# First mixer of a hybrid model block: float32 products on unsplit weights in place of three split products, modulation on TensorE, silu on ScalarE, the last projection by token halves

## The chip, the cores and the metric

One core of one Trainium2 chip runs the whole program. The metric is the device time of one execution in microseconds (us), lower is better. The times of a kernel are taken on several executions and their median is compared; the profile is of one execution of its own.

## What is computed

The input is 256 tokens of 1024 float32 features. The program has two blocks, each a mixer followed by a mixture of experts of its own kind (the first with 32 experts, four of them per token). All of it is float32. Only the first mixer concerns this study; cut to what matters:

```python
shift, scale, gate, ... = split(silu(c) @ ada_w + ada_b)         # modulation, 6 x 1024
h = rmsnorm(x, norm1_g) * (1 + scale) + shift
proj = h @ w_in                                     # gdn_qkv, gdn_z, ssd_z, ssd_xbc, small columns
qkv = silu(causal_dwconv(gdn_qkv, gdn_conv_w))      # four taps
q, k = l2norm(...), l2norm(...)
o = gated_delta_rule_chunked(q, k, v, beta, g)      # 4 chunks of 64 tokens, one after the other
o = rmsnorm(o, gdn_norm_g) * silu(gdn_z)
xbc = silu(causal_dwconv(ssd_xbc, ssd_conv_w) + ssd_conv_b)
y = ssd_chunked(...) + ssd_d * xs
y = rmsnorm(y * silu(ssd_z), ssd_norm_g)            # in two groups
x = x + gate * (concatenate([o, y]) @ w_out)
# then: norm2, router logits, experts
```

## The kernel before

The chip's engines work beside each other: TensorE (PE) multiplies matrices, VectorE (DVE), ScalarE (ACT) and GpSimd (POOL) do the rest, and the queue of SyncE (SP) issues the loads of weights. All weights come from HBM once, in chunks of 128 partitions x 2048 float32 (1 MB). The class `Stream` hands them out: a list `todo` in the order of use, a number of slots in SBUF, and a load is issued (L173) as soon as its turn has come and a slot of its phase (A is the first mixer, B its experts) is free. In phase A there are N1 = 4 slots; for phase B come six of ring1 when the mixer ends and five of the pool pB, 15 in all.

*Start (0 to about 36 us).* `ada_first` (L448 and around) computes the first third of the modulation on PE: for each of eight chunks four matmuls of 512 columns, each in a group of 32 of the array's columns, summed over the chunks. Meanwhile x is normalised and transposed to `h32`.

*Projections.* The mixer has 34 projection chunks: 6 for the SSD convolution input, 8 for q and k, 4 for ssd_z, 4 for v, 4 for gdn_z, 4 + 4 for the output. Each is 256 output columns wide and makes 16 products (8 blocks of the contraction by two halves). PE has a fast format, fp32r, with fewer bits; to keep the accuracy both operands are split in a high and a low part. `splitter` (L364 and around) does this for a weight chunk in four parts: ACT copies a part into `wh` in fp32r, then DVE or POOL (the table SPD says which) makes `wl` = w - wh. `h` is split in the same way into `hT`, and the inputs of the output projection into the pairs `cs` and `cg`. One product is then three fp32r matmuls:

```python
mm(o, l[0], r[0], start=start, stop=False)
mm(o, l[0], r[1], start=False, stop=False)
mm(o, l[1], r[0], start=False, stop=stop)
```

The slot of a chunk is given back when it is split, and one chunk is split ahead of use (`Stream.get`).

*Modulation batches 1 and 2* (`ada_batch`, L463): eight chunks each, multiplied and summed on DVE (L479, 128x2048 each), then a product with ones on PE adds over the partitions. They lie beside the projections.

*What follows a projection.* `conv_silu`: ACT takes the first tap from PSUM, DVE the three others (L661), ACT a tanh, DVE the last step (L664): silu(z) as (tanh(z/2) + 1) * z/2, with the halves folded into the weights. Then PE transposes the result, ACT copies it. For the two gates the same by `twice_silu` and in `emit_z`.

*Order.* It is set by generators that give up their turn at each piece: `weave` runs a main generator, and after each of its turns so much of the side generators as their rates say (FILL1, FILL2 for the projections beside a main chain, RA for the modulation). In turn: the SSD projections; the q and k projections beside `ssd`; `gdn_prep` (around L900 to L950), the inverse of 64x64 triangular blocks by doubling, in blocks of 32 (matmuls of Xc, Yc, Qc, with Xc the transposed of Yc by DVE, L927), beside ssd_z and v; `gdn_steps`, the chain over four chunks of 64 tokens, beside gdn_z and the SSD half of the output projection. What is left of the side work runs after the chain. Then the GDN outputs `o` are transposed, multiplied with norm weight and gate, split, and the GDN half of the output projection runs for both halves of the tokens (128 each) of each of four chunks; `router_logits` takes each result, adds it to x (L1202 transposes it) and multiplies with the router's weights. The experts' first product, `ps_gu<-w,xe`, follows at 426 us. Behind the mixer nothing is changed.

Of the kernel before, what the change touches and what calls it, by code (L numbers as in the profile page):

```python
# [12 lines left out]
F32 = mybir.dt.float32  # L13
# [104 lines left out]
class Stream:  # L118
# [151 lines left out]
def kernel_body(ctx, tc, ins, consts, out):  # L270
# [78 lines left out]
    pA = Sides(tc, "pA", {"a4", "wh", "wl", "vT", "cf", "gb0", "gh", "ssx", "jkx", "ss", "rsv", "rsq", "rs"})  # L349
# [4 lines left out]
    SP.dma_start(x, ins["x"].rearrange("o (t p) d -> p (o t) d", p=P))  # L354
    ws.ring(pw, N1 - 3, ph)

# [21 lines left out]
    ws.splitter = splitter(pA)  # L378
    k.spd = SPD[0]

# [82 lines left out]
    def ada_batch(b):  # L463
# [26 lines left out]
        ws.give(slot)  # L490
# [54 lines left out]
    nc.vector.tensor_scalar(col_w, pb[:, :144], 0.5, None, op0=ALU.mult)  # L545
    hb = pA.tile([P, 12], F32, name="hb")
    nc.vector.tensor_scalar(hb, colv("ssd_conv_b"), 0.5, None, op0=ALU.mult)
# [16 lines left out]
    ws.ring(pB, N2 - NR1, {"B": N2 - NR1})  # L564
    block1_moe(k, pB)
    ws.close(pB)
    pB_cm.__exit__(None, None, None)
    ps_cm.__exit__(None, None, None)
# [18 lines left out]
def mixer1(k):  # L587
    nc, tc, ws, pA = k.nc, k.tc, k.ws, k.pA
    mm, mm3, tt, act, bank, C, ident = k.mm, k.mm3, k.tt, k.act, k.bank, k.C, k.ident
    Cb = k.Cb  # L590
    split_into = k.split_into
    hT, h32, ro, col_w, hb, colv = k.hT, k.h32, k.ro, k.col_w, k.hb, k.colv
# [5 lines left out]
    def a4r(name):  # L598
        return pA.tile([P, 1024], F32R, tag="a4", bufs=NA4, name=name)
# [52 lines left out]
    def conv_silu(pj, wc, ct, nct, dst, bias=None):  # L652
# [9 lines left out]
        th = pA.tile([P, T], F32, tag="cv_t", bufs=2, name="cv_t")  # L662
        act(th, y, AF.Tanh)
        V.scalar_tensor_tensor(dst, th, 1.0, y, op0=ALU.add, op1=ALU.mult)  # L664

    def proj_ch(n, emit, emit2=None):

        for i in range(n):
            w = ws.get(split=True)
# [14 lines left out]
    def proj_tok(n, l, emit):  # L684

        for i in range(n):
            w = ws.get(split=True)
            pj = bank("pj", PJ)
            for t in range(2):
                for kk in range(KD):  # L690
                    sl = slice(kk * 256, kk * 256 + 256)
# [1838 lines left out]
```

## Time and profile before

| | |
|---|---|
| time, median of 3 executions | 2185.27 us (2173.07 to 2186.01) |
| the profiled execution's own time | 2186.19 us |
| its span (first to last instruction) | 2184.4 us |
| first mixer, from the start to the first gate_up product | 426 us |
| PE busy, over the span | 89% |
| DVE / ACT / POOL busy, over the span | 32% / 20% / 12% |
| HBM read | 703.70 MB |

The span and the time differ by what lies before and after the first and last instruction. PE busy means that a matmul was under way, at whichever clock; the granted clock is a mean over a stretch, as a share of full speed. The rows come from one execution.

### The profile page before, as it was taken

How to read it: one execution, taken by the hardware profiler on the slowest of the kernel's cores; microseconds unless marked ns; L12 is line 12 of the kernel's file. 1: busy time of each engine (PE TensorE's matmuls, PEld its weight loads, DVE VectorE, ACT ScalarE, POOL GpSimd, SP SyncE). 2: the span in 40 equal slices, each digit the busy share in tenths (PEclk: the TensorE clock that was granted, in tenths of full speed). 3: DMA queues.
4: the chain of work that ended last, by engine and by line, in shares of the span. 5: the costliest groups of instructions: out<-in, count | busy, mean ns of one | idle time of the engine just before them, and what ended most of it. 6: DMA issues, size and time to landing. Idle time of an engine off the chain costs nothing. (4 is left out here: it accounts for less than half of the span.)

```text
span 2184.4 us, 27466 instructions
## 1 busy us (share of the span) xinstructions
PE 1942.8 (89%) x11276; PEld 1035.2 (47%) x11277; DVE 695.8 (32%) x1438; ACT 436.5 (20%) x1030; POOL 256.9 (12%) x206
## 2 busy tenths in 40 slices
PE   6888899799999999989999999879999887776777
PEld 3877878633343434334343333378779531212111
DVE  4988847421111111111211111374765200001001
ACT  3655424211010101001010000132444210101001
POOL 2524212100000000000000000242434000000000
PEclk9999879999999999999999999989999899998999
DMA  8654415789999999988999999926238699999997
GB/s 309 212 174 136 150 66 174 293 349 391 411 420 421 421 421 406 388 363 353 414 418 416 422 393 422 359 92 193 78 87 334 273 420 421 420 421 371 421 421 290
DMA packets 170747, 706.67 MB, mean 324 GB/s; under 512 B 20775, under 2 KB 83796, under 8 KB 95860
## 3 DMA queue, kind: packets, MB, share of 16 engines
q1 hardware_dynamic: 170612, 704.80, 81.4%
q8 instruction: 93, 1.52, 0.3%
q14 instruction: 42, 0.34, 0.0%
HBM read 703.70 MB, written 1.05 MB: 323 GB/s over the span
## 5 line engine op out<-in xcount | busy, mean ns | idle before, releaser
L283 PE MATMUL ps_gu<-w,xe 128*64 128x512 f32 (+1 forms) x3072 | 693.0, 629 | 82.2 <-DMA w<-in_w_up_dram 36.6
L283 PEld LDWEIGHTS ps_gu<-w,xe 128*64 128x64 f32 (+1 forms) x3072 | 228.9, 132 | 524.7 <-issue 398.0
L283 PE MATMUL ps_y<-w,aT 128*64 128x512 f32 (+1 forms) x1536 | 383.9, 599 | 13.8 <-DMA w<-in_w_down_dram 13.0
L283 PEld LDWEIGHTS ps_y<-w,aT 128*64 128x64 f32 (+1 forms) x1536 | 116.5, 127 | 234.0 <-issue 182.9
L293 POOL TENSOR_TENSOR wl<-w,wh 128x512 fp32r<-128x512 f32 x126 | 179.5, 1433 | 387.1 <-ACT wh L296 382.8
L1579 DVE TENSOR_SCALAR g<-ps_gu 128x512 f32<-128x512 f32 x32 | 22.0, 686 | 490.2 <-PE ps_gu L283 490.2
L296 ACT ACTIVATE g<-g 128x512 f32<-128x512 f32 x32 | 20.2, 630 | 694.7 <-DVE g L1579 694.7
L296 ACT ACTIVATE wh<-w 128x512 fp32r<-128x512 f32 x244 | 139.4, 622 | 88.1 <-PE ps_pj L283 51.9
L283 PE MATMUL ps_pj<-hT,wh 128*128 128x256 f32 x704 | 146.4, 304 | 7.5 <-DVE cv_y L661 3.5
L293 DVE TENSOR_TENSOR wl<-w,wh 128x512 fp32r<-128x512 f32 x118 | 116.1, 1002 | 48.1 <-ACT wh L296 47.4
L283 PEld LDWEIGHTS ps_pj<-hT,wh 128*128 128x128 f32 x704 | 119.4, 205 | 13.4 <-issue 5.7
L293 DVE TENSOR_TENSOR x<-x,ps_g 128x512 f32<-128x512 f32 x96 | 66.0, 687 | 173.9 <-PE ps_g L283 173.9
L283 PE MATMUL ps_pj<-hT,wl 128*128 128x256 f32 x352 | 107.0, 304 | 4.9 <-DVE wl L293 2.5
L283 PE MATMUL ps_g<-ys,sgT 128*128 128x512 f32 x192 | 93.7, 617 | 1.7 <-DVE ys L293 0.8
L283 PE MATMUL ps_g<-selr,xo 128*128 128x256 f32 x320 | 76.7, 394 | 18.3 <-ACT selr L296 15.3
L293 DVE TENSOR_TENSOR a<-g,ps_gu 128x512 f32<-128x512 f32 x8 | 5.5, 687 | 239.3 <-PE ps_gu L283 239.3
L283 PEld LDWEIGHTS ps_g<-selr,xo 128*128 128x128 f32 x320 | 56.8, 192 | 47.8 <-ACT selr L296 23.3
L283 PEld LDWEIGHTS ps_pj<-hT,wl 128*128 128x128 f32 x352 | 72.6, 206 | 6.9 <-DVE wl L293 2.8
L283 PE MATMUL ps_pj<-uT,wh 128*128 128x256 f32 x384 | 72.8, 291 | 0.0
L283 PEld LDWEIGHTS ps_pj<-uT,wh 128*128 128x128 f32 x384 | 61.4, 197 | 4.2 <-issue 3.7
L293 DVE TENSOR_TENSOR ys<-ps_y,gb 128x512 f32<-128x512 f32 x32 | 22.1, 692 | 129.3 <-PE ps_y L283 129.3
L1381 DVE COPY aT<-ps_g 128x512 f32<-128x512 f32 x16 | 11.1, 692 | 159.2 <-PE ps_g L1376 159.2
(533 smaller groups left out, 2137.0 us busy)
## 6 DMA issues: line engine op xcount, KB each, us to landing
w<-in_moe_w_gu_dram SPq DMA_DIRECT2D x256, 1024.0 KB, 12.6
w<-in_moe_w_down_dram SPq DMA_DIRECT2D x120, 1024.0 KB, 16.2
w<-in_w_gate_dram SPq DMA_DIRECT2D x64, 1024.0 KB, 19.8
w<-in_w_up_dram SPq DMA_DIRECT2D x64, 1024.0 KB, 19.8
w<-in_w_down_dram SPq DMA_DIRECT2D x64, 1024.0 KB, 19.8
w<-in_w_in_dram SPq DMA_DIRECT2D x45, 1024.0 KB, 5.2
w<-in_ada_w_dram SPq DMA_DIRECT2D x24, 1024.0 KB, 5.1
w<-in_w_out_dram SPq DMA_DIRECT2D x12, 1024.0 KB, 6.1
```

What stands on the lines that cost most here:

```text
L283: return nc.tensor.matmul(o, l, r, start=start, stop=stop)
L293: (eng or nc.vector).tensor_tensor(o, a, b, op=op)
L296: nc.scalar.activation(o, i, f, **kw)
L1381: k.nc.vector.tensor_copy(dst, pt)
L1579: V.tensor_scalar(g, gu[j], 7.0, None, op0=ALU.min)
```

## The change

- The projections take the float32 chunk as it lies in its slot, and float32 activations: one matmul for each product in place of three. `wh`, `wl`, `hT` and the split pairs `cs`, `cg` are gone, and with them the work of `splitter` in this mixer (the second mixer keeps it, with the same values of SPD). A chunk keeps its slot until its products are issued.
- The two later modulation batches are made on PE like the first one: 64 matmuls of 512 columns, then four transposes and two products that pick a row.
- silu is one ScalarE function in place of tanh and a DVE step; the halves that were folded in are gone.
- A pool `pq` adds four slots to phases A and B (8 in A); pB has one slot in place of five, so that B has 15 as before. No more than four chunks are live until the small vectors (`rowsA`) are under way.
- The GDN half of the output projection runs by halves of the tokens: the first half (`first_tile`) beside the last steps of the chain, the second after it. Its four chunks keep their slots until the second half has used them. The router's logits are taken by halves, too. FILL2 is 1.05.

```diff
+    def raw(self):
+
+        self.fill()
+        return self._next("mm")
...
+    pq_cm = tc.tile_pool(name="pq", bufs=NQ)
+    pq = pq_cm.__enter__()
...
+    ws.limit(N1)
     ws.ring(pw, N1 - 3, ph)
+    ws.ring(pq, NQ, {"A": NQ, "B": NQ})
...
-        acc = None
+        pm = None
         for kk in range(KD):
             while not ws.ready():
                 yield
             w = ws.get()
-            if acc is None:
-                acc = w
-                slot = ws.take()
-                nc.vector.tensor_scalar(acc, w, cact[:, 0:1], None, op0=ALU.mult)
-            else:
-                nc.vector.scalar_tensor_tensor(acc, w, cact[:, kk:kk + 1], acc, op0=ALU.mult, op1=ALU.add)
-                ws.done()
+            pm = pm or bank()
+            for j in range(4):
+                mm(pm[32 * j:32 * j + 32], cb[:, kk], w[:, j * 512:(j + 1) * 512], start=(kk == 0), stop=(kk == KD - 1))
...
+        mr = pA.tile([P, 512], F32, tag="t2b", bufs=2, name="mr")
+        act(mr, pm, AF.Copy)
         pt = bank()
-        for j in range(8):
-            mm(pt[:, j:j + 1], acc[:, c0 + j * P:c0 + j * P + P], C("ones"))
-        tt(mcol[:, 8 + 8 * b:16 + 8 * b], pt[:, :8], colv("ada_b1")[:, 8 * b - 8:8 * b], ALU.add)
+        for q in range(4):
+            nc.tensor.transpose(pt[:, q * P:(q + 1) * P], mr[:, q * P:(q + 1) * P], ident)
+        v = lambda a: a.rearrange("p (j q) -> p q j", j=2)
+        tt(v(mcol[:, 8 + 8 * b:16 + 8 * b]), pt.rearrange("p (q j r) -> p q j r", q=4, r=32)[:, :, c0 // 512:c0 // 512 + 2, 0],
+           v(colv("ada_b1")[:, 8 * b - 8:8 * b]), ALU.add)
         for n in range(2):
+            r = 32 * (g0 // 512 + n)
             pg = bank()
-            mm(pg, Cb("ones"), acc[:, g0 + n * 512:g0 + n * 512 + 512])
+            mm(pg, ident[:, r:r + 1].to_broadcast([P, P]), mr)
...
+    ws.limit(99)
...
-    hT = [pA.tile([P, KD, T], F32R, name=f"hT{i}") for i in range(2)]
     for kk in range(KD):
         h = h32[kk // 4][:, kk % 4]
         nc.vector.tensor_scalar(h, h, a1[:, kk:kk + 1], mcol[:, kk:kk + 1], op0=ALU.mult, op1=ALU.add)
-        split_into(h, hT[0][:, kk], hT[1][:, kk], eng=nc.gpsimd if kk % 2 else None)
...
+    ws.ring(pB, NB, {"B": NB})
...
-        th = pA.tile([P, T], F32, tag="cv_t", bufs=2, name="cv_t")
-        act(th, y, AF.Tanh)
-        V.scalar_tensor_tensor(dst, th, 1.0, y, op0=ALU.add, op1=ALU.mult)
+        act(dst, y, AF.Silu)
...
-                    sl = slice(kk * 256 + ct * P, kk * 256 + ct * P + P)
-                    mm3(pj[:, ct * T:(ct + 1) * T], (w[0][:, sl], w[1][:, sl]), (hT[0][:, kk], hT[1][:, kk]), start=(kk == 0), stop=(kk == KD - 1))
+                    c0 = kk * 256 + ct * P
+                    mm(pj[:, ct * T:(ct + 1) * T], w[:, c0:c0 + P], h1(kk), start=(kk == 0), stop=(kk == KD - 1))
...
+            ws.give(slot)
...
-            g2 = twice_silu(pj)
+            g2 = pA.tile([P, 512], F32, tag="t2a", bufs=2, name="hs")
+            act(g2, pj, AF.Silu)
...
-            cf = pA.tile([P, T], F32, tag="cf", bufs=2, name="cf")
-            act(cf, pt[:, :T], AF.Copy, scale=colv("ssd_norm_g")[:, c:c + 1])
-            split_into(cf, cats[c // 4][0][:, c % 4], cats[c // 4][1][:, c % 4])
+            act(cats[c // 4][:, c % 4], pt[:, :T], AF.Copy, scale=colv("ssd_norm_g")[:, c:c + 1])
...
+                    done[0] = hg == 1
...
+        act(zs[i // 2][:, (i % 2) * 2:(i % 2) * 2 + 2], pj.rearrange("p (a b) -> p a b", a=2), AF.Silu)
...
+    def gdn_cat(t):
+        for hg in range(2):
+            pt = bank()
+            for i in range(4):
+                h = hg * 4 + i
+                nc.tensor.transpose(pt[:, i * P:(i + 1) * P], o[t][:, h * P:(h + 1) * P], C("swap"))
+            sl = slice(t * P, (t + 1) * P)
+            V.scalar_tensor_tensor(catg[hg][:, :, sl], pt.rearrange("p (c s) -> p c s", c=4), gh, zs[hg][:, :, sl], op0=ALU.mult, op1=ALU.mult)
+
+    def gdn_out(t, emit):
+        for i in range(4):
+            if t == 0:
+                c = ws.raw()
+                while c is None:
+                    yield
+                    c = ws.raw()
+                held.append(c)
+            w, slot = held[i]
+            pj = bank("pj", PJ)
+            for kk in range(KD):
+                mm(pj[:, :256], catg[kk // 4][:, kk % 4, t * P:(t + 1) * P], w[:, kk * 256:(kk + 1) * 256], start=(kk == 0), stop=(kk == KD - 1))
+            if t:
+                ws.give(slot)
+            emit(i, t, pj[:, :256])
+            yield
...
+    def first_tile():
+        yield from ada2
+        r.extend(router())
+        while not done[0]:
+            yield
+        catg.extend(catp("cg"))
+        gdn_cat(0)
+        yield
+        yield from gdn_out(0, r[0].tile)
+
+    r, done = [], [False]
+    fill = chain(proj_ch(4, None, emit_z), ssd_out, first_tile())
     weave(gdn_steps(), (fill, FILL2), (ada2, RA[3]))
-    run_all(fill, ada2)
+    run_all(fill)
...
-    k.spd = SPD[4]
...
-    catg = catp("cg")
-    for h in range(8):
...
-        split_into(cf, catg[h // 4][0][:, h % 4], catg[h // 4][1][:, h % 4])
...
-    emit, logits = router_logits(k, pA, add, lambda: pA.tile([P, 256], F32, tag="cf", bufs=2, name="xT"), k.rw, 32)
-    run_all(proj_tok(4, lambda part, kk, t: catg[kk // 4][part][:, kk % 4, t * P:(t + 1) * P], emit))
-    logits(k.lg, k.cr)
-
+    gdn_cat(1)
+    run_all(gdn_out(1, r[0].tile))
+    r[1](k.lg, k.cr)
...
+    def emit_t(i, t, o):
+        sl = slice(i * 256, (i + 1) * 256)
+        add(t, sl, o)
+        if t not in pl:
+            pl[t] = k.bank()
...
-SPD = ((1, 2),) * 3 + ((1, 2, 3), (1, 3), (), (1, 2), (1, 2))
+SPD = ((), (1, 2), (1, 2))
 RA = (0.34, 0.4, 0.25, 0.3)
 FILL1 = 0.8
-FILL2 = 0.6
+FILL2 = 1.05
 N1 = 4
-N2 = 11
+NQ = 4
+NB = 1
```

Three places show how the rows of the queues move. First DVE, in the doubling steps of the inverse: `Yc` is brought up to date, `Xc` is its transposed, which PE waits for; `cs`, `wl` are splits, `w<-w,cact` a step of the modulation, `cv_y` the taps of a convolution. Before:

```order
L293 TENSOR_TENSOR Yc<-Yc,ps_g 128x256
L293 TENSOR_TENSOR cs_2366<-cf,cs_2365 128x256 x2
L927 STREAM_TRANSPOSE Xc<-Yc 128x256
L479 SCALAR_TENSOR_TENSOR w<-w,cact 128x2048
L661 SCALAR_TENSOR_TENSOR cv_y<-ps_pj,col_w,cv_y 128x255
L293 TENSOR_TENSOR wl<-w,wh 128x512
L661 SCALAR_TENSOR_TENSOR cv_y<-ps_pj,col_w,cv_y 128x254
L293 TENSOR_TENSOR wl<-w,wh 128x512
L661 SCALAR_TENSOR_TENSOR cv_y<-ps_pj,col_w,cv_y 128x253
L664 SCALAR_TENSOR_TENSOR vT<-cv_t,cv_y 128x256
```

After:

```order
L294 TENSOR_TENSOR Yc<-Yc,ps_g 128x256
L933 STREAM_TRANSPOSE Xc<-Yc 128x256
L662 SCALAR_TENSOR_TENSOR cv_y<-ps_pj,col_w,cv_y 128x255
L662 SCALAR_TENSOR_TENSOR cv_y<-ps_pj,col_w,cv_y 128x254
L662 SCALAR_TENSOR_TENSOR cv_y<-ps_pj,col_w,cv_y 128x253
```

The transpose stands directly behind the update, and the splits, the modulation step and the last step of silu (L664) are gone from the queue.

Second PE, at the last GDN step (`vn,dT` is its last product): `cs` products are the SSD half of the output projection, `cg` the GDN half, `o` the chain's result, `rw,xT` the router's logits, `w,c_64` and `c_64,w` the sums over the partitions of a modulation batch. Before:

```order
L283 MATMUL ps_g<-c_64,w 128x1 x8
L283 MATMUL ps_g<-w,c_64 128x512 x2
L283 MATMUL ps_g<-vn,dT 64x128 x4
L283 MATMUL ps_pj<-wh,cs_2365 128x256
L283 MATMUL ps_pj<-wl,cs_2365 128x256
L283 MATMUL ps_pj<-wh,cs_2366 128x256
L283 MATMUL ps_pj<-wh,cs_2365 128x256
```

After:

```order
L284 MATMUL ps_g<-rw,xT 128x32 x2
L284 MATMUL ps_pj<-w,cg_2881 128x256 x3
L1232 MATMUL ps_g<-c_64,x 128x128 x2
L284 MATMUL ps_g<-vn,dT 64x128 x3
L284 MATMUL ps_g<-rw,xT 128x32 x2
L284 MATMUL ps_g<-vn,dT 64x128 x5
L1127 MATMUL ps_g<-ca,o_2394 128x128 x4
L284 MATMUL ps_pj<-w,cg_2880 128x256 x2
L1127 MATMUL ps_g<-ca,o_2394 128x128 x4
L284 MATMUL ps_pj<-w,cg_2880 128x256 x3
L284 MATMUL ps_pj<-w,cg_2881 128x256 x4
L284 MATMUL ps_pj<-w,cg_2880 128x256 x3
```

Before, the SSD half is still to come behind the last step and the GDN half behind that; after, the SSD half and most of the first token half of the GDN products lie ahead of the last step, and the second half follows it.

Third ACT, at the first convolutions: `cv_y` is the first tap, `cv_t` a tanh, `xT` a silu, `ea` an exponential, `sp_e` and `sp_z` the exponential and logarithm of the softplus; ACT_TABLE_LOAD loads the functions that the next activation needs. Before:

```order
L296 ACTIVATE cv_y<-ps_pj,hb,col_w 128x256
L296 ACTIVATE cv_t<-cv_y 128x256
L296 ACTIVATE cv_y<-ps_pj,hb,col_w 128x256
L296 ACTIVATE ea<-rowsA 128x24
L296 ACTIVATE cv_t<-cv_y 128x256
L296 ACTIVATE cv_y<-ps_pj,hb,col_w 128x256
L296 ACTIVATE sp_e<-sp_e 128x64
L296 ACT_TABLE_LOAD
L296 ACTIVATE sp_z<-sp_u 128x64
L296 ACT_TABLE_LOAD
L296 ACTIVATE cv_t<-cv_y 128x256
L296 ACTIVATE cv_y<-ps_pj,hb,col_w 128x256
```

After:

```order
L297 ACTIVATE cv_y<-ps_pj,col_a,col_w 128x256
L297 ACT_TABLE_LOAD
L297 ACTIVATE xT<-cv_y 128x256
L297 ACTIVATE cv_y<-ps_pj,col_a,col_w 128x256
L297 ACT_TABLE_LOAD
L297 ACTIVATE ea<-rowsA 128x24
L297 ACT_TABLE_LOAD
L297 ACTIVATE xT<-cv_y 128x256
L297 ACT_TABLE_LOAD
L297 ACTIVATE sp_e<-sp_e 128x64
L297 ACTIVATE cv_y<-ps_pj,col_a,col_w 128x256
L297 ACT_TABLE_LOAD
```

In this piece six loads stand where two stood; up to the experts' first product the queue has 20 where it had 5.

## Rows read from the trace of the kernel before

**Rows 1.** The page's first part: busy us, share of span, instructions of each engine.

```profile
PE 1942.8 (89%) x11276; PEld 1035.2 (47%) x11277; DVE 695.8 (32%) x1438; ACT 436.5 (20%) x1030; POOL 256.9 (12%) x206
```

**Rows 2.** Windows by stage: start:end, us, PE PEld DVE ACT POOL busy, PEclk, DMA, GB/s.

```profile
0.00:36.00 36.00, 17.64 (x86) 5.49 (x88) 9.31 (x29) 11.18 (x22) 4.33 (x9) 1.00 0.94 354
36.00:196.00 160.00, 141.96 (x1005) 126.05 (x1005) 137.69 (x246) 90.73 (x252) 63.84 (x47) 0.93 0.56 184
196.00:290.00 94.00, 79.21 (x1833) 72.64 (x1833) 74.85 (x132) 37.68 (x90) 33.34 (x22) 0.90 0.46 148
290.00:364.00 74.00, 74.00 (x508) 62.58 (x506) 41.07 (x110) 28.95 (x79) 10.57 (x7) 0.85 0.25 84
364.00:414.00 50.00, 44.68 (x358) 41.97 (x356) 33.38 (x76) 17.53 (x47) 12.61 (x9) 1.00 0.66 255
414.00:426.00 12.00, 4.81 (x24) 4.08 (x24) 7.69 (x46) 2.80 (x9) 2.15 (x2) 0.70 0.83 338
```

**Rows 3.** Windows of 10 us around the end of the mixer and in the experts.

```profile
400.00:410.00 10.00, 9.28 (x76) 8.83 (x76) 4.35 (x8) 2.32 (x9) 1.02 (x1) 1.00 0.30 109
480.00:490.00 10.00, 10.00 (x28) 2.57 (x30) 3.29 (x6) 0.00 (x0) 0.00 (x0) 0.66 0.46 161
560.00:570.00 10.00, 10.00 (x48) 3.98 (x45) 0.00 (x0) 0.00 (x0) 0.00 (x0) 1.00 1.01 421
```

**Rows 4.** Waits of PE, 0 to 435 us: total us, times, longest us.

```profile
PE ps_g L283 <- DMA w<-in_ada_w_dram: 9.6, 5, 3.5
PE ps_g L809 <- DVE qk L664: 5.7, 3, 4.6
...
PE ps_pj L283 <- ACT hT L296: 3.2, 1, 3.2
```

**Rows 5.** Groups of instructions, 36 to 196 us: busy us, mean ns, idle before.

```profile
L293 POOL TENSOR_TENSOR wl<-w,wh 128x512 fp32r<-128x512 f32 x33 | 49.4, 1501 | 89.5 <-ACT wh L296 85.6 <-PE ps_pj L283 4.0
L296 ACT ACTIVATE wh<-w 128x512 fp32r<-128x512 f32 x65 | 38.1, 626 | 8.7 <-PE ps_pj L283 6.5 <-issue 1.7 <-DMA w<-in_w_in_dram 0.4
L293 DVE TENSOR_TENSOR wl<-w,wh 128x512 fp32r<-128x512 f32 x34 | 32.9, 977 | 2.1 <-ACT wh L296 1.5 <-issue 0.6
L479 DVE SCALAR_TENSOR_TENSOR w<-w,cact 128x2048 f32<-128x2048 f32 x7 | 16.4, 2341 | 0.0
```

**Rows 6.** Timeline of PE, out-projection: start us, us, engine line op.

```profile
404.14 0.40 PE L283 MATMUL ps_pj<-wh,cg 128*128 128x256 f32 x2
404.38 0.28 PE L283 MATMUL ps_pj<-wl,cg 128*128 128x256 f32 x1
...
407.67 0.28 PE L283 MATMUL ps_pj<-wh,cg 128*128 128x256 f32 x1
```

**Rows 7.** Timeline of PE in the expert stage: a train of float32 products.

```profile
515.17 5.57 PE L283 MATMUL ps_g<-selr,xo 128*128 128x256 f32 x24
520.57 0.61 PE L1310 MATMUL ps_g<-c,sg 128*128 128x128 f32 x4
```

**Rows 8.** The same train as a window (columns as in rows 2).

```profile
515.17:520.57 5.40, 5.40 (x25) 4.19 (x25) 0.00 (x0) 2.82 (x5) 0.00 (x0) 1.00 1.02 419
```

**Rows 9.** Timeline of PE in the start: chunks of the first modulation batch.

```profile
9.71 1.94 PE L283 MATMUL ps_g<-w,cb 128*32 128x512 f32 x8 [0.44 <-DMA w<-in_ada_w_dram]
...
26.34 1.92 PE L283 MATMUL ps_g<-w,cb 128*32 128x512 f32 x16
```

**Rows 10.** Timeline of PE in the GDN steps: small matmuls between products.

```profile
309.32 0.43 PE L283 MATMUL ps_g<-r,Y 64*64 64x128 f32 x2
309.68 0.38 PE L283 MATMUL ps_pj<-hT,wh 128*128 128x256 f32 x1
309.91 0.28 PE L283 MATMUL ps_pj<-hT,wl 128*128 128x256 f32 x1
```

**Rows 11.** Timeline of ACT at the softplus.

```profile
56.66 1.28 ACT L296 ACT_TABLE_LOAD   x1
57.96 0.26 ACT L296 ACTIVATE sp_z<-sp_u 128x64 f32<-128x64 f32 x1
```

**Rows 12.** Timeline of PE where the first mixer ends.

```profile
426.08 8.48 PE L283 MATMUL ps_gu<-w,xe 128*64 128x512 f32 x32
```

More of the change, by code (lines that the diff above doesn't have):

```diff
@@ L544, in kernel_body @@
     nc.tensor.transpose(pb[:, 96:144], sw2, ident[:48, :48])
-    nc.vector.tensor_scalar(col_w, pb[:, :144], 0.5, None, op0=ALU.mult)
-    hb = pA.tile([P, 12], F32, name="hb")
-    nc.vector.tensor_scalar(hb, colv("ssd_conv_b"), 0.5, None, op0=ALU.mult)
+    nc.vector.tensor_copy(col_w, pb[:, :144])
     a2 = pc.tile([P, KD], F32, name="a2")
@@ L596, in a4, with h1 @@
         return pA.tile([P, 1024], F32, tag="a4", bufs=NA4, name=name)
-    def a4r(name):
-        return pA.tile([P, 1024], F32R, tag="a4", bufs=NA4, name=name)
+    def h1(kk):
+        return h32[kk // 4][:, kk % 4]
     pb = bank()
@@ L661, in conv_silu, with chunks @@
             V.scalar_tensor_tensor(y[:, s:], pj[:, :T - s], w(3 - s), y[:, s:], op0=ALU.mult, op1=ALU.add)
-        th = pA.tile([P, T], F32, tag="cv_t", bufs=2, name="cv_t")
-        act(th, y, AF.Tanh)
-        V.scalar_tensor_tensor(dst, th, 1.0, y, op0=ALU.add, op1=ALU.mult)
-    def proj_ch(n, emit, emit2=None):
-        for i in range(n):
-            w = ws.get(split=True)
+        act(dst, y, AF.Silu)
+    def chunks(n):
+        for i in range(n):
+            c = ws.raw()
+            while c is None:
+                yield None
+                c = ws.raw()
+            yield i, *c
+    def proj_ch(n, emit, emit2=None):
+        for c in chunks(n):
+            if c is None:
+                yield
+                continue
+            i, w, slot = c
             pj = bank("pj", PJ)
@@ L684, in proj_tok @@
     def proj_tok(n, l, emit):
-        for i in range(n):
-            w = ws.get(split=True)
+        for c in chunks(n):
+            if c is None:
+                yield
+                continue
+            i, w, slot = c
             pj = bank("pj", PJ)
@@ L953, in catp @@
     def catp(nm):
-        return [[a4r(f"{nm}{i}{p}").rearrange("p (c s) -> p c s", c=4) for p in range(2)] for i in range(2)]
+        return [a4(f"{nm}{i}").rearrange("p (c s) -> p c s", c=4) for i in range(2)]
     cats = []
@@ L967, in emit @@
                     act(jk, ys[t][:, g * 512:(g + 1) * 512], AF.Square, accum_out=ssy[:, t * 2 + g:t * 2 + g + 1])
-        yield from proj_tok(4, lambda part, kk, t: hT[part][:, kk, t * P:(t + 1) * P], emit)
+        yield from proj_tok(4, lambda kk, t: h1(kk)[:, t * P:(t + 1) * P], emit)
         rsy = pA.tile([P, 4], F32, name="rsy")
-        k.rstd(rsy, ssy, 0.25 / 512, pA, "rsy")
+        k.rstd(rsy, ssy, 1.0 / 512, pA, "rsy")
         for t in range(2):
@@ new lines, in mixer1, with add, router @@
+    gh = colv("gdn_norm_g")
+    catg, held = [], []
+    def add(t, sl, o):
+        d = pA.tile([P, 256], F32, tag="vT", bufs=2, name="d")
+        tt(d, o, gb[0][:, sl])
+        tt(x[:, t, sl], x[:, t, sl], d, ALU.add)
+    def router():
+        V.scalar_tensor_tensor(k.a2, k.mcol[:, 24:32], 1.0, colv("norm2_g"), op0=ALU.add, op1=ALU.mult)
+        pt = bank()
+        for kk in range(KD):
+            mm(pt[:, :32], k.mcol[:, 16 + kk:17 + kk].to_broadcast([P, P]), k.rw[:, kk], start=(kk == 0), stop=(kk == KD - 1))
+        tt(k.cr, pt[:, :32], k.rb, ALU.add)
+        tt(k.rw, k.rw, k.a2[:, :, None].to_broadcast([P, KD, 32]))
+        return router_logits(k, pA, add, lambda: pA.tile([P, 256], F32, tag="cf", bufs=2, name="xT"), k.rw, 32)
@@ L1148, in cols @@
     def cols(w, c0, n):
-        return [(w[:, c:c + 256].rearrange("(k p) n -> p k n", p=P), (8, 256), None, True) for c in range(c0, c0 + n, 256)]
+        return [(w[:, c:c + 256].rearrange("(k p) n -> p k n", p=P), (8, 256), None, "mm") for c in range(c0, c0 + n, 256)]
     def mixed(main, side, every):
@@ L1192, in router_logits @@
     x, nc = k.x, k.nc
-    pl = [k.bank() for _ in range(2)]
+    pl = {}
     ssx = pool.tile([P, 2, 4], F32, name="ssx")
+    def emit_t(i, t, o):
[3 more added lines that the diff above has]
+            pl[t] = k.bank()
+        pt = k.bank()
+        for j in range(2):
+            nc.tensor.transpose(pt[:, j * P:(j + 1) * P], x[:, t, i * 256 + j * P:i * 256 + j * P + P], k.ident)
+        xT = tile()
+        if t:
+            k.act(xT, pt[:, :256], AF.Copy)
+        else:
+            nc.vector.tensor_copy(xT, pt[:, :256])
+        for j in range(2):
+            mi = k.mm(pl[t][:, :n], xT[:, j * P:(j + 1) * P], rw[:, i * 2 + j], start=(i == 0 and j == 0), stop=(i == 3 and j == 1))
+        k.act(tile(), x[:, t, sl], AF.Square, accum_out=ssx[:, t, i:i + 1])
+        if i == 3 and t and WARM2[0]:
+            k.warm(WARM2[0], mi, k.ca[:, 0:512])
     def emit(i, pj):
-        sl = slice(i * 256, (i + 1) * 256)
         for t in range(2):
-            add(t, sl, pj[:, t * 256:(t + 1) * 256])
-            pt = k.bank()
-            for j in range(2):
-                nc.tensor.transpose(pt[:, j * P:(j + 1) * P], x[:, t, i * 256 + j * P:i * 256 + j * P + P], k.ident)
-            xT = tile()
-            if t:
-                k.act(xT, pt[:, :256], AF.Copy)
-            else:
-                nc.vector.tensor_copy(xT, pt[:, :256])
-            for j in range(2):
-                mi = k.mm(pl[t][:, :n], xT[:, j * P:(j + 1) * P], rw[:, i * 2 + j], start=(i == 0 and j == 0), stop=(i == 3 and j == 1))
-            k.act(tile(), x[:, t, sl], AF.Square, accum_out=ssx[:, t, i:i + 1])
-        if i == 3 and WARM2[0]:
-            k.warm(WARM2[0], mi, k.ca[:, 0:512])
+            emit_t(i, t, pj[:, t * 256:(t + 1) * 256])
+    emit.tile = emit_t
     def logits(dst, bias):
```

70 lines of the change are left out of this document (21 added, 49 removed).

## Prediction

> **What bounds the kernel now.** I read the page's busy shares first: TensorE (PE) works 89% of the span [rows 1], so the question is whether it is PE's work or its waits that set the changed stretch. The table by stage comes next [rows 2]. The change touches only the first mixer, which ends where the first expert's gate_up product starts, at 426 us. Up to 36 us the DMA is the limit (share 0.94). From 36 to 414 us PE is busy 141.96 + 79.21 + 74.00 + 44.68 = 339.9 of 378 us: 38 us of waits, and the rest work, part of it at the low clock (granted 0.93, 0.90, 0.85, 1.00). VectorE (DVE) is nearly as full in the first of these stages, 137.69 of 160 us. The list of what PE waits for [rows 4] names the culprits: modulation weights from HBM 9.6 us, the silu result qk on DVE 5.7 us, the split of hT 3.2 us, and many small ones.
>
> Does a shift of the mixer's end reach the total? In the expert stage the weights stream at 421 GB/s, but at 400 to 410 and at 480 to 490 us the DMA share is only 0.30 and 0.46 [rows 3]: the weight slots are full and the stream stands still until PE has used one. So I let a microsecond of the mixer be a microsecond of the total. The profiled execution took 2186.19 us, 0.9 above the median of 2185.27; the sum is made against 2186.19. About 1% (21.9 us) is what a measurement of this kernel tells from no change.
>
> **Part by part.**
>
> *Products.* 34 chunks of 16 products each = 544. Before, one product is three fp32r records: ten products lie between 404.14 and 407.67 us [rows 6], 0.353 us each. After, it is one float32 product, two records of 256 columns each. The expert stage shows this shape: 24 records from 515.17 to 520.57 [rows 7], 0.450 a product; the window's own row counts 25 records [rows 8], by which it is 0.432. I take 0.44: 544 x (0.44 - 0.353) = +47 us (bounds +43 and +53).
>
> *Modulation on PE.* Two batches of eight chunks leave DVE, where one chunk is a 128x2048 instruction of 2.34 us [rows 5], and go to PE, four 512-column matmuls in four column groups. The first batch already does it so: two chunks in 1.92 us at the high clock, one in 1.94 at the low one [rows 9]. 16 x 0.96 = +15 us (bounds +15 and +31); the transposes and the row products that follow take the place of 16 products with a vector of ones and two of 512 columns, and are set at nothing.
>
> *Waits that go.* The split went over ScalarE (ACT), DVE and GpSimd (POOL): from 36 to 196 us 65 copies by 0.626 on ACT, 34 subtractions by 0.977 on DVE, 33 by 1.50 on POOL, and 7 modulation steps [rows 5]. DVE gets 33 + 16 = 49 us lighter in that stage alone, ACT 38. The order shows what PE's operands stood behind: in the inverse two splits stand between the update of Yc and its transposed Xc, which PE needs for the next doubling, and behind Xc a modulation step of 2.34 us and two wl splits among the taps of the convolution; after, nothing stands between and the taps follow each other. Of the 38 us I take three quarters away, -29 (bounds 0 and -38): the waits for the dependent chain itself (convolution, silu, transpose) stay.
>
> *Clock.* A granted mean of 0.93 lies between two levels, 1.2 and 2.4 GHz; the time at the lower is 2 x (0.07 x 160 + 0.10 x 94 + 0.15 x 74) = 63 us [rows 2], which costs at most half, 32. The granted clock was 1.00 where PE had products close together, 364 to 414 us, and less where small matmuls or waits filled the time. With denser work I take back half: -16 (bounds 0 and -32).
>
> *Small matmuls between products.* From 308.4 to 311.9 products and pairs of 64-row matmuls alternate, and the product after such a pair takes 0.38 where its neighbour takes 0.28 [rows 10], 0.1 more. The order has as many such changes after as before (212 for 214 in the mixer), so I take -4 (bounds 0 and -9).
>
> *Start.* hT's split goes with its 3.2 us [rows 4]; eight slots in place of four let modulation loads run ahead, which only matters once the DMA is no longer at 0.94. -3 (bounds 0 and -10).
>
> *Tail.* Before, the last out-projection runs after all GDN steps with both token halves. After, the first half lies beside the steps, and after the last one only four chunks x 8 products = 32 remain, but the norm of the last tile stands bare in front of them, with less left to lie beside it; 12 us from 414 to 426 (PE busy 4.8) stay as they were [rows 2]. The difference of all this beyond the products counted above: +6 (bounds 0 and +20).
>
> *At nothing.* Dropping the halvings and hb: a few instructions on engines with room. The four out-projection chunks that keep their slots until the second half delay the expert loads queued behind them on SP; between the last step and the first gate_up (426.08 before, [rows 12]) there lie 32 x 0.44 + 12 = 26 us, and a chunk of 1.05 MB at 420 GB/s [rows 3] is 2.5 us, so four slots given back late (10 us of loads) are covered; without that cover it would be up to 10. Taking POOL's work away (10.6 to 63.8 us a stage) gives nothing of its own, its waits being in the term above.
>
> Sum: +47 + 15 - 29 - 16 - 4 - 3 + 6 = **+16**, 2186 + 16 = **2202 us**.
>
> **The new wait.** Silu replaces tanh plus a DVE step, but up to the first gate_up ACT's queue has 20 table loads where it had 5. A load took 1.28 us, and the next activation began 0.02 us after it [rows 11]. What is queued behind a waiting silu on ACT: the next convolution's first step, the copies of transposed tiles, exponentials for decay; PE's transposes wait for these. 15 x 1.28 = 19 us of ACT, against 38 us of copies that leave it in the one stage: in the forecast this is covered.
>
> **Rivals.**
> - *DVE was the real limit* of the first 250 us. For it: 137.69 of 160 us busy. Against: PE is as full. Then only 4 of 38 us of waits stay, the clock comes back in full and the changes get cheaper: +43 + 15 - 34 - 32 - 9 - 10 = -27, **2159 us**. Chance 0.24.
> - *The table loads set the pace* (slower). Silu alternates with exponential and logarithm on the ACT queue, so that nearly every convolution pays a load in front of the silu that PE's transpose waits for. Then of the waits 23 go and 19 come back: +47 + 15 - 4 - 16 - 3 + 6 = +45, **2231 us**. It decides from five loads on the path: five times 1.28 = 6.4 carry the forecast over +21.9. For it: the order puts a load ahead of both silus of the first chunk. Against: ACT is at 90.73 of 160 us and gets lighter, and PE has other products to take. Chance 0.25. The Trainium skill, "ScalarE: Activation LUTs", section "What ACT_TABLE_LOAD costs", counts 2.66 us for a switch, 1.28 for the load and 1.38 for a drain, and its section "Table sets: the hidden batching unit" advises to group functions by set; by that it would be 15 x 2.66 = 40 in place of 19 and 2252 us. The trace agrees on the load and shows no drain before the next activation.
> - *The shift is swallowed* by the expert stage, whose stream at 421 GB/s [rows 3] would set its end whatever the mixer does: **2186 us**. Against it stand the two windows with a halted stream. Chance 0.11.
>
> **How the numbers follow.** The forecast has 0.40; its own range is 2186 to 2218, of which 0.12 lies over +1%. Faster by over 1% (below 2163): 0.22 of the first rival. Slower (over 2207): 0.12 + 0.25 = 0.37. Within: 0.02 + 0.28 + 0.11 = 0.41. The range for 8 in 10 goes from just below the first rival's time, 2157, to a little above the second's, 2235.
>
> **What would show it.** Right: one product at 0.43 to 0.45 us in the profile after; PE waits from 36 us to the first gate_up near 10 us; granted clock over 0.95 in the stages that had 0.85 to 0.93; the first gate_up near 442 us; everything after it as long as before. Wrong: waits of PE on silu results (xT, qk, vT) of more than 15 us; a product outside 0.43 to 0.45; the granted clock unchanged, which alone gives 16 us back; or a first gate_up that has moved and a total that has not, which would be the third rival.

## The result and the profile after

The changed kernel takes 2199.23 us (median of 11 runs, 2194.53 to 2207.54), the kernel before 2185.27 (2170.42 to 2188.11 in the same comparison): a ratio of 1.0075, 95% interval 1.0057 to 1.0093. It is slower by 14 us, where 2202 and +16 were forecast; both lie within 1%. The profiled execution has a span of 2197.5 us, 13.1 more than before.

The page's first part for the kernel after, the columns as in [rows 1]:

```profile
PE 1974.3 (90%) x10836; PEld 1019.6 (46%) x10837; DVE 561.6 (26%) x1276; ACT 379.5 (17%) x887; POOL 159.8 (7%) x142
```

PE has 31 us more, DVE lost 134, ACT 57, POOL 97. What the three engines lost, 288 us between them, did not make up in the total for what PE gained.

Windows of the kernel after, cut where the stages end (first product, GDN preparation, first GDN step, last step, gate_up), columns as in [rows 2]:

```profile
0.00:33.70 33.70, 17.57 (x85) 5.36 (x86) 5.19 (x24) 6.79 (x12) 0.40 (x6) 0.85 0.93 358
33.70:191.70 158.00, 156.41 (x750) 116.07 (x750) 72.53 (x172) 72.36 (x190) 9.37 (x8) 0.99 0.62 204
191.70:294.50 102.80, 94.82 (x1798) 72.48 (x1797) 39.39 (x90) 23.94 (x58) 13.02 (x12) 0.97 0.44 145
294.50:401.10 106.60, 105.52 (x631) 86.05 (x630) 35.79 (x108) 20.60 (x66) 5.07 (x4) 0.99 0.28 99
401.10:425.00 23.90, 18.96 (x85) 16.00 (x86) 9.71 (x37) 4.66 (x21) 1.04 (x1) 0.76 0.65 267
425.00:437.50 12.50, 5.51 (x27) 4.35 (x26) 7.00 (x43) 3.45 (x8) 1.04 (x1) 0.69 1.02 380
```

Against [rows 2] with the same cuts (first product at 35.8, preparation from 196.5, first step at 289.6, gate_up at 426.1 us): the first product comes 2 us sooner, the stage of the SSD, q and k projections takes 158.0 in place of 160.7 us although PE makes eight chunks of modulation in it, the preparation takes 102.8 for 93.1, and from the first GDN step to gate_up it is 143.0 for 136.5. PE idles 1.6 + 8.0 + 1.1 + 4.9 = 15.6 us from 33.7 to 425, where it idled 38. DVE fell from 137.69 busy to 72.53 in the stage of the projections. The granted clock rose to 0.97 to 0.99, but for the last 36 us, where it is 0.76 and 0.69. In the start it reads 0.85 where [rows 2] has 1.00, although PE's chunks take the same time there in both kernels; the last section comes back to this.

What PE waits for in the kernel after (0 to 450 us; total us, times, longest):

```profile
PE ps_g L284 <- DMA w<-in_ada_w_dram: 9.5, 5, 3.5
PE ps_g L284 <- issue: 8.6, 5, 3.6
PE ps_g L284 <- DVE selm L1641: 4.2, 1, 4.2
PE ps_g L1127 <- DVE rs_q L400: 4.0, 1, 4.0
...
PE ps_g L284 <- ACT xT L297: 0.5, 1, 0.5
```

The silu results and the splits of [rows 4] are gone from the list (the `xT` in its last line is the router's, at 428 us); the modulation loads of the start stay (they belong to the first batch). New is L1127: the transposes of the last tile's result wait 4.0 us for its norm.

The timeline of PE after, at the places of the sum: a modulation chunk, eight products of a GDN step's filling, the last step, the end of the mixer.

```profile
309.34 1.06 PE L284 MATMUL ps_g<-w,cb 128*32 128x512 f32 x8
310.34 1.09 PE L284 MATMUL ps_g<-S,qk 128*64 128x128 f32 x16
...
316.04 3.72 PE L284 MATMUL ps_pj<-h,w 128*128 128x256 f32 x16
319.69 1.08 PE L284 MATMUL ps_g<-r,Y 64*64 64x128 f32 x8
...
398.90 2.19 PE L284 MATMUL ps_g<-vn,dT 64*64 64x128 f32 x10
...
405.09 1.08 PE L1127 MATMUL ps_g<-ca,o 128*128 128x128 f32 x4 [4.00 <-DVE rs_q L400]
...
437.49 8.36 PE L284 MATMUL ps_gu<-w,xe 128*64 128x512 f32 x32
```

A chunk of modulation takes 1.00 us, a product between small matmuls 3.65 / 8 = 0.456. At this place the small matmuls of a GDN step stand in trains of 8 or 16 behind whole trains of products; in [rows 10] pairs of them alternated with single records. gate_up moved from 426.08 [rows 12] to 437.49, by 11.4 us, and 1760 us follow it, 1758 before.

### The profile page after: what moved, and what is told of

Same layout as the page of the kernel before. It is cut to its first block, busy times and chain, and to the rows that moved or that the text cites. A ratio compares the mean times of both kernels' runs of the same rounds, so it can differ in the third digit from the quotient of the medians.

```text
span 2197.5 us, 26095 instructions
## 1 busy us (share of the span) xinstructions
PE 1974.3 (90%) x10836; PEld 1019.6 (46%) x10837; DVE 561.6 (26%) x1276; ACT 379.5 (17%) x887; POOL 159.8 (7%) x142
## 3 DMA queue, kind: packets, MB, share of 16 engines
HBM read 703.70 MB, written 1.05 MB: 321 GB/s over the span
## 5 line engine op out<-in xcount | busy, mean ns | idle before, releaser
L284 PE MATMUL ps_pj<-h,w 128*128 128x256 f32 x704 | 171.1, 392 | 1.0 <-DVE h L542 1.0
L284 PEld LDWEIGHTS ps_pj<-h,w 128*128 128x128 f32 x704 | 131.5, 195 | 31.8 <-issue 11.6
L294 POOL TENSOR_TENSOR wl<-w,wh 128x512 fp32r<-128x512 f32 x66 | 89.2, 1361 | 131.3 <-ACT wh L297 131.3
L297 ACT ACTIVATE wh<-w 128x512 fp32r<-128x512 f32 x108 | 60.9, 622 | 51.5 <-PE ps_pj L284 32.5
L662 DVE SCALAR_TENSOR_TENSOR cv_y<-ps_pj,col_w,cv_y 128x255 f32<-128x255 f32 (+2 forms) x108 | 51.8, 480 | 59.9 <-ACT cv_y L297 57.6
L284 PEld LDWEIGHTS ps_g<-ys,sgT 128*128 128x128 f32 x192 | 31.1, 188 | 64.1 <-issue 36.0
L294 DVE TENSOR_TENSOR wl<-w,wh 128x512 fp32r<-128x512 f32 x42 | 45.9, 1119 | 36.6 <-ACT wh L297 36.6
L284 PE MATMUL ps_pj<-uT,wl 128*128 128x256 f32 x192 | 55.2, 288 | 0.0
```

Source lines behind the costliest of these rows:

```text
L284: return nc.tensor.matmul(o, l, r, start=start, stop=stop)
L294: (eng or nc.vector).tensor_tensor(o, a, b, op=op)
L297: nc.scalar.activation(o, i, f, **kw)
L662: V.scalar_tensor_tensor(y[:, s:], pj[:, :T - s], w(3 - s), y[:, s:], op0=ALU.mult, op1=ALU.add)
```

## The experiments

Twelve kernels were run. Ratios are to the kernel before, timed beside each of them (its medians there were 2180.5 to 2185.3 us). Where two of these kernels were timed at different times, the difference of their medians carries up to 5 us of this shift; the difference of their ratios does not. The profiles are of one execution each: from the first gate_up to the end, where nothing was changed, they show 1748 to 1766 us (leaving out the one run that chose other experts).

**Products twice for q and k.** The edit, with rep=2 for the eight chunks:

```diff
-                for kk in range(KD):
+                for kk in list(range(KD)) * rep:
```

> The changed kernel with every product chain of the eight q and k chunks issued twice (the second pass writes the same sums over the first): 128 more float32 products and nothing else. If PE's work is what the first mixer's length is made of, they cost 128 x 0.44 = 56 us: 2199 + 56 = 2255 us. If the chain of convolution, silu and copies set the pace of that stage, much would lie beside it: under +30, below 2229. If the expert stage swallowed what the mixer adds: 2199.

Measured: 2251.25 us, ratio 1.0304 (1.0253 to 1.0354), 52 us more than the changed kernel. The end of the mixer in its timeline:

```profile
493.55 8.45 PE L284 MATMUL ps_gu<-w,xe 128*64 128x512 f32 x32
```

It moved by 493.55 - 437.49 = 56.06 us, 0.438 for each of 128 products, and nearly all of it arrived in the total. So work added on PE lengthens that stage of the changed kernel in full, and the expert stage swallows little of it: the third rival falls.

**Modulation back on DVE.**

```diff
-            for j in range(4):
-                mm(pm[32 * j:32 * j + 32], cb[:, kk], w[:, j * 512:(j + 1) * 512], ...)
...
+                nc.vector.scalar_tensor_tensor(acc, w, cact[:, kk:kk + 1], acc, op0=ALU.mult, op1=ALU.add)
```

> The changed kernel with modulation batches 1 and 2 back on DVE (sixteen steps of 2.34 us, sums over the partitions on PE as before). If PE bounds the mixer, PE gets 16 x 0.96 = 15 us less, of which some 5 come back as waits behind the long DVE steps: 2199 - 10 = 2189 us. If DVE's company was what made PE wait in the kernel before, the waits return and it is 2199 or more.

Measured: 2189.00 us, ratio 1.0025 (1.0001 to 1.0048), 10 us less than the changed kernel, as expected. Its first stage, in a window:

```profile
34.40:182.50 148.10, 144.79 (x697) 115.53 (x697) 92.05 (x182) 71.29 (x189) 11.40 (x8) 0.99 0.66 223
```

DVE has 92 of 148 us and PE idles only 3.3: the long DVE steps hide once the splits are gone, and the stage is 158.0 - 148.1 = 9.9 us shorter. The first gate_up came at 428.86 us, 8.6 sooner.

**silu by tanh.**

```diff
-        act(dst, y, AF.Silu)
...
+        act(th, y, AF.Tanh)
+        V.scalar_tensor_tensor(dst, th, 1.0, y, op0=ALU.add, op1=ALU.mult)
```

> The changed kernel with silu by tanh and a DVE step as in the kernel before; the 15 additional table loads on ACT are gone, 36 more DVE steps are there. If the loads are covered, as PE's waits on silu results in the profile after say (0.5 us), the time is 2199 within 4. If the loads set the pace it falls by half to all of their 19 us: 2180 to 2190.

Measured: 2197.00 us, ratio 1.0072 (1.0039 to 1.0105): no difference to the changed kernel. The group of table loads in the kernel after, up to 437 us, and two rows of ACT's timeline there:

```profile
L297 ACT ACT_TABLE_LOAD x20 | 25.7, 1283 | 7.6 <-DVE cv_y L662 4.9 <-DVE m L777 1.7 <-PEq L2550 0.6
```

```profile
48.82 1.28 ACT L297 ACT_TABLE_LOAD   x1 [1.64 <-DVE cv_y L662]
50.12 0.42 ACT L297 ACTIVATE xT<-cv_y 128x256 f32<-128x256 f32 x1
```

20 loads took 25.7 us; the kernel before and this run have five up to there (the piece of ACT's order shown ahead holds five of the 20, not six). None of it shows in the time. The run also adds 36 DVE steps (15.5 us in all), so what it shows is that loads and steps come to the same; that the loads cost PE nothing rests also on the list of its waits, which names no silu result. ACT was busy 72.36 of 158 us in the projections. The second rival falls.

**Without the low parts, first try.** The kernel before, with the high part of a chunk in place of its low part, so that `wl` is never computed:

```diff
+            return hi, hi
...
-    ws.splitter = splitter(pA)
+    ws.splitter = highs(pA)
```

> The kernel before, with the low parts of the weights of the first mixer not computed (the high part is used in their place: that part of the sum is left out); the three fp32r matmuls, ACT's copies and the modulation on DVE stay. PE's instructions are the same, DVE and POOL lose their 68 + 68 subtractions. If these subtractions in the queues made the waits and the low clock of the kernel before, 22 us of waits and some 24 us of clock come back: 2185 - 40 = 2145 us. If the waits belong to ACT's copies and the dependent chain, and the clock to the kind of matmuls, it falls by less than 15: over 2170.

Measured: 2575.00 us, ratio 1.1798. The total says nothing here: with the high part in both places the projections come out near double, and other expert weights were read (728.87 MB from HBM in place of 703.70). The mixer's end can be compared:

```profile
399.84 7.80 PE L283 MATMUL ps_gu<-w,xe 128*64 128x512 f32 x32
```

It came 26.2 us sooner than in [rows 12], between the 40 that my reading gave and the under 15 of the rival. So the run was made again with other operands.

**Without the low parts, second try.** The third matmul takes the low part of the activations once more:

```diff
-                    mm3(pj[...], (w[0][:, sl], w[1][:, sl]), (hT[0][:, kk], hT[1][:, kk]), ...)
+                    for j, a in enumerate((0, 1, 1)):
+                        mm(pj[...], w[0][:, sl], hT[a][:, kk], ...)
```

> The kernel before, without the low parts of the weights of the first mixer; in the third matmul of a product the low part of the activations is taken once more, so that the terms with the low weights are left out and the values stay close. As in the run without low parts, where the mixer ended 26 us sooner than in the kernel before: 2185 - 26 = 2159 us, which is what the subtractions on DVE and POOL cost PE in waits and clock. If their place in the queues did not matter: 2185.

Measured: 2159.96 us, ratio 0.9896 (0.9852 to 0.9940), 23 us below the kernel before. Its first two stages:

```profile
35.10:178.40 143.30, 136.91 (x988) 123.34 (x989) 106.68 (x217) 88.05 (x248) 17.71 (x13) 0.94 0.64 214
178.40:272.30 93.90, 82.45 (x1853) 76.32 (x1851) 52.31 (x110) 39.17 (x95) 11.65 (x12) 0.88 0.42 137
```

With the same instructions on PE the first stage took 143.3 in place of 160.7 us. That is what the subtractions in DVE's and POOL's queues cost PE; the preparation did not gain. The GDN steps took 69.8 us at a granted clock of 0.89, where [rows 2] has 74.0 at 0.85. So the splits did hold PE up, and the changed kernel got this back, but for more than it was worth.

**Modulation on PE in the kernel before**, the second edit the other way round, on the kernel before:

```diff
-                nc.vector.scalar_tensor_tensor(acc, w, cact[:, kk:kk + 1], acc, op0=ALU.mult, op1=ALU.add)
...
+            for j in range(4):
+                mm(pm[32 * j:32 * j + 32], cb[:, kk], w[:, j * 512:(j + 1) * 512], ...)
```

> The kernel before with modulation batches 1 and 2 on PE as in the changed kernel, nothing else. PE gets 15 us more, DVE 37 us less. If DVE's load made PE's waits and low clock in the first stages, half of 26 us or more comes back and it is 2185 + 15 - 13 to - 26 = 2174 to 2187 us. If PE alone counts: 2200.

Measured: 2189.20 us, ratio 1.0017 (0.9997 to 1.0037): no difference that can be told, 2 us above what was expected if DVE's load counts and 11 us under what PE alone would give. The mixer ended where it ended before, and its projections took 155.3 us in place of 160.7, with PE idle for 10.5 in place of 18.5:

```profile
424.97 8.42 PE L283 MATMUL ps_gu<-w,xe 128*64 128x512 f32 x32
```

```profile
35.20:190.50 155.30, 144.85 (x1014) 119.91 (x1014) 120.62 (x239) 88.21 (x245) 57.41 (x44) 0.96 0.57 190
```

So most of the 15 us on PE were paid for by the relief of DVE, in the kernel with splits; in the changed kernel, whose DVE is half idle, 10 of them stay unpaid.

**The last projection whole.**

```diff
-    fill = chain(proj_ch(4, None, emit_z), ssd_out, first_tile())
+    fill = chain(proj_ch(4, None, emit_z), ssd_out)
...
-    run_all(gdn_out(1, r[0].tile))
+    run_all(proj_tok(4, lambda kk, t: catg[kk // 4][:, kk % 4, t * P:(t + 1) * P], r[0]))
...
-FILL2 = 1.05
+FILL2 = 0.6
```

> The changed kernel with the GDN half of the output projection whole again: both token halves after the last step, FILL2 0.6 as before, so that the SSD half of the output projection lies partly behind the last step and beside the last norm. The prediction put the tail by halves at +6, of which the profile after shows 4.0 us of PE waiting for the norm of the last tile. If that is right: 2199 - 4 = 2195 us, and no such wait. If the halves gain more than that by filling the steps: 2203 or more.

Measured: 2187.95 us, ratio 1.0023 (0.9998 to 1.0048), 11 us less than the changed kernel, where 4 were expected. The stretch after the last step, as a window of each kernel, first the changed one, then this one:

```profile
395.00:425.00 30.00, 23.99 (x113) 19.79 (x112) 11.66 (x41) 6.07 (x27) 1.04 (x1) 0.77 0.52 212
```

```profile
369.30:419.90 50.60, 49.98 (x260) 43.32 (x260) 16.43 (x46) 5.71 (x23) 3.80 (x3) 1.00 0.63 249
```

By halves PE idles 6 of 30 us and the granted clock is 0.77; whole, it idles 0.6 of 50.6 at 1.00. The wait for the norm is only a part of the price. The granted clock stood at its lower level from 399.1 to 412.8 us of the changed kernel:

```profile
399.14:412.78 13.64, 8.69 (x29) 6.89 (x28) 7.84 (x32) 3.22 (x16) 1.04 (x1) 0.50 0.24 86
```

PE worked 8.7 us there, which at the upper level would have taken about half: an estimate of 4 us from this row. But the clock fell in the last step's own products, behind a wait of 1.07 us for the sum with x and 2 us ahead of the wait for the norm (401.1 to 405.1), so that wait did not make it fall. All four profiles with halves show the bare norm (4.0 to 4.8 us) and the low level beside it, in one of them beginning only in the wait; the three with the last projection whole show no wait over 0.5 us there. What makes the clock fall is not shown. In the two profiles the mixer ends 6.05 us apart (431.44 and 437.49); the other 5 us of the medians lie behind the mixer, and why they do is not shown.

**Whole, with the faster fill.** Two things differed in that run, the place of the products and the rate FILL2, so here is one of them alone (the edit is against that run):

```diff
-FILL2 = 0.6
+FILL2 = 1.05
```

> The changed kernel with the GDN half of the output projection whole and behind the last step, but FILL2 left at 1.05: the gdn_z and SSD products are used up sooner beside the steps, and less of them lies beside the last norm. With FILL2 0.6 the whole projection took 2188 us, the changed kernel 2199. If the halves (chunks held, a bare norm) are what costs, this is 2188 too. If it is the pace of the fill, with the steps running out of products and the norm bare, it is 2195 to 2200.

Measured: 2185.51 us, ratio 1.0037 (1.0012 to 1.0062); the median is near the 2188 expected of the halves and outside 2195 to 2200, but four of its twelve executions took 2196 to 2203. Its interval just touches that of the changed kernel; by the ratios it is 8 us below it, by the medians 14. So the halves are the likelier cause and not a settled one.

**Both together.** The changed kernel with modulation on DVE and the last projection whole (the two edits above).

> The changed kernel with modulation back on DVE and the last projection whole: of the change the float32 products without any split and silu on ScalarE stay. Alone the two edits gave 10 and 11 us. If they are independent: 2199 - 21 = 2178 us, so the float32 products by themselves are 7 us better than the kernel before, not worse. If the two gains are the same one (a PE freed at the same place): 2188.

Measured: 2181.01 us, ratio 1.0010 (0.9988 to 1.0031). By the medians 18 of the 21 us came, by the ratios 14 of 22. In the profile the first gate_up came at 418.38 us, 19.1 sooner than in the changed kernel, where the two edits alone gave 8.6 and 6.05. The two prices are therefore separate ones in the main, though the times alone do not settle it. But float32 products without splits, with silu on ACT, are as fast as the kernel before, not 7 us better.

**Float32 products for the SSD, q and k projections alone**, in the kernel before:

```diff
+            c = ws.raw()
...
+                    mm(pj[:, ct * T:(ct + 1) * T], w[:, c0:c0 + P], h32[kk // 4][:, kk % 4], ...)
...
-    weave(proj_ch(6, emit), (ada1, RA[0]))
+    weave(raw_ch(6, emit), (ada1, RA[0]))
+    k.split_h()
```

> The kernel before with float32 products on unsplit weights for the 14 chunks of the SSD, q and k projections alone (and h split after the first six of them); the 20 later chunks stay split, modulation stays on DVE, silu by tanh, the last projection whole. With modulation on DVE the changed kernel took 148 us from the first product to the GDN preparation, the kernel before 161; the later stages took 246 and 230. If each stage keeps its own: 2185 - 13 = 2172 us. If the relief of the first stage is only moved to the next: 2185 or more.

Measured: 2169.78 us, ratio 0.9945 (0.9922 to 0.9968), faster than both kernels. Windows of its first stage and of the GDN steps:

```profile
34.30:189.70 155.40, 152.21 (x764) 122.73 (x765) 114.11 (x225) 64.53 (x199) 24.85 (x19) 0.96 0.59 198
...
278.60:343.90 65.30, 65.30 (x512) 55.26 (x509) 41.45 (x110) 28.93 (x79) 10.57 (x7) 0.97 0.30 98
```

The first stage gained 5 us, less than the 13 expected, and the GDN steps, in which nothing was changed, 9: 65.3 us at a clock of 0.97, where [rows 2] has 74.0 at 0.85. The two runs that follow have the same float32 products ahead of the same steps; there the steps look like this:

```profile
284.62:356.09 71.47, 71.47 (x517) 60.90 (x515) 41.34 (x110) 29.08 (x79) 10.56 (x7) 0.88 0.27 88
289.54:360.32 70.78, 70.32 (x509) 59.50 (x507) 41.16 (x110) 28.97 (x79) 8.91 (x7) 0.89 0.27 89
```

So the 9 us belong to this one execution at least in part, and are not shown to come from the edit.

**The same with silu on ACT in the convolutions.**

```diff
-        act(th, y, AF.Tanh)
-        V.scalar_tensor_tensor(dst, th, 1.0, y, op0=ALU.add, op1=ALU.mult)
+        act(dst, y, AF.Silu, scale=2.0)
```

> The run with float32 products for the SSD, q and k projections alone (2170 us), with silu on ScalarE in the convolutions (scale 2 on the halved taps) in place of tanh and a DVE step; the gates keep tanh. DVE had 114 of 155 us in the first stage there and PE waited 3.1 us on it for qk and 3.3 for vT. If these waits are what the DVE step costs: 2164 to 2167 us. If the table loads take their place: 2170 or more.

Measured: 2165.61 us, ratio 0.9933 (0.9911 to 0.9955): within what was expected, but the interval overlaps that of the run without it, so these 4 us are not shown. Its runs spread from 2159.89 to 2182.59, and the profile is of the longest of them.

**The same (with tanh) with ssd_z unsplit as well.**

```diff
-    order += mixed(cols(w_in, 4112, 1024) + ...
+    order += mixed(cols(w_in, 4112, 1024, "mm") + ...
...
-        yield from proj_tok(4, lambda part, kk, t: hT[part][:, kk, t * P:(t + 1) * P], emit)
+        yield from raw_tok(4, lambda kk, t: h32[kk // 4][:, kk % 4, t * P:(t + 1) * P], emit)
```

> The same run (2170 us) with the four ssd_z chunks unsplit as well, in the GDN preparation, where DVE and ACT were busy 70 and 40 of 89 us and PE waited 11 us in all. PE gets 4 x 16 x (0.44 - 0.353) = 5.6 us more and 16 subtractions leave the queues. If PE's work is the limit there too: 2170 + 5 = 2175 us. If the splits are: 2165 or less.

Measured: 2178.57 us, ratio 0.9986 (0.9960 to 1.0011), 9 us more than without it, where PE's work alone said 5 and the splits' company said a gain. The two intervals just touch. In the profiles the preparation is 105.3 us here, 88.9 in the run without, and 100.1 in the run with silu, whose preparation has the same products as the run without (the projections ahead of it took 150.1, 155.4 and 150.6); so part of this difference is not the edit's. That the unsplit products cost in the preparation is likely and not settled.

## Why the prediction was right, point by point

- *Products, +47.* Right. A product took 0.438 us at the margin and 0.456 between small matmuls, for 0.44 taken; 544 x (0.438 - 0.353) = 46. The 0.456 lies a little outside the 0.43 to 0.45 that was named as a sign.
- *Modulation on PE, +15.* Right as work (1.00 us a chunk for 0.96 taken). What it is worth came out at 10 in the changed kernel and, in the kernel before, at 4 by the ratio (6 between the medians, 8 at the interval's end); the price of work on PE depends on what it takes off the engine that PE waits for.
- *Waits, -29.* 22 came back (38 to 15.6 us idle, where near 10 was named as a sign). The 15.6 hold 4.9 from the last tile's stage, which the sum has in the tail; without them it is 27 of the 29. The direction rests on the second run without low parts; the chain of convolution, silu and transpose, which I expected to stay, is hardly seen after, and what stayed is the norm and the preparation: 8.0 us idle, 7.7 of them with nothing in the profile that PE waited for.
- *Clock, -16.* Under-sized outside the tail: the time at the lower level fell from 63 to 2 x (0.01 x 158 + 0.03 x 102.8 + 0.01 x 106.6) = 11.5 us, worth up to 26. The profile shows the clock beside PE's denser work; that the one made the other was not tried by itself.
- *Tail, +6.* The mechanism was right, a bare norm of the last tile (4.0 us); its size is not settled: with the fill changed too it cost 11 us in the medians and 6 in the profiles, with the fill left as it was 8 by the ratios. Beside the wait stood the low clock, by the row an estimate of 4 us, which the step left out.
- *Small matmuls, -4, and start, -3.* The start gave 2. The first was not measured by itself.
- *The sum.* Over the whole mixer PE's busy time, added up from the windows, rose from 362.3 us [rows 2] to 398.8, by 36.5, and its idle time fell from 63.7 to 38.7, by 25: together the 11.5 us by which the first gate_up moved. Products and modulation are 46 + 15 = 61 us of work, so clock and small matmuls gave back 24.5 between them, net of what the low clock of the tail cost; -20 was forecast for the two. The rows do not divide it further. The first gate_up moved by 11.5 us for the 16 forecast. That the time came within 3 is partly luck: single terms missed by about as much, in both directions (clock and small matmuls gave back more, the waits less, the tail cost more), and the unchanged rest of the program differs from one profile to another by up to 18 us.
- *At nothing.* Right for the table loads, by the run with tanh. What the chunks held for the halves cost was not separated.
- *The rivals.* That DVE was the real limit is half true: its subtractions and POOL's held up PE for 23 us, but the step to float32 products, modulation and halves costs 46 + 10 and some 6 to 11. Table loads as the pace, and a shift swallowed by the experts, were shown wrong.

The experiments that beat both kernels leave the first 14 chunks unsplit and the 20 later ones split, with modulation on DVE and the last projection whole: 2169.78 us, and 2165.61 with silu on ACT. DVE's share does not by itself say where to split: in the kernel before it was busy 86% of the projection stage, where unsplit products paid, and 80% of the preparation, where they seem to cost [rows 2].

## What to carry to other kernels

A change that relieves three engines and loads the fourth is judged on the fourth alone, at its price per instruction, and then credited with the waits that go. Choose for each stage by itself, and by a run: 14 chunks unsplit beat both the kernel with all 34 split and the one with none. Where a critical engine idles a few microseconds, look at its granted clock on both sides of the gap: the price can be larger than the wait, and the clock can have fallen before it. Before a gain of a stage is put down to an edit, look at the same stage in other runs.

## What the runs showed of the hardware that was not expected

- The GDN steps with split products ran at granted clocks from 0.85 (74.0 us, the kernel before) to 0.97 (65.3 us, the run with float32 products for the SSD, q and k projections), each in one profiled execution. Two more runs with the same products ahead of them lie between (71.5 and 70.8 us), so that an earlier stage sets this clock is not shown.
- 20 table loads of 1.28 us each on ACT, alternating with silus, exponentials and logarithms, changed the time of the kernel by no more than the measurement's noise (2199.23 with them, 2197.00 with five loads and 36 more DVE steps).
- In the start the granted clock of a profile can read higher than the instructions show. From 20 to 24 us PE does the same work in the same time in both kernels, a modulation chunk in 1.94 us where later ones take 1.0, and the clock reads 1.00 before and 0.50 after. So the slow chunk of [rows 9] was at the lower level, as the prediction reads it, though [rows 2] has 1.00 for the whole start, and the 0.85 of the kernel after is no loss. First the kernel before, then the one after:

```profile
20.00:24.00 4.00, 3.48 (x14) 1.19 (x15) 0.94 (x2) 0.01 (x1) 0.00 (x0) 1.00 0.99 412
20.00:24.00 4.00, 3.46 (x14) 1.18 (x15) 0.96 (x2) 0.00 (x0) 0.00 (x0) 0.50 0.98 406
```
